# A diffusion layer on one core: the last modulation block by TensorE alone, and GLA's steps of a head moved

## The chip, the cores and the metric

The kernel runs on one core of one Trainium2 chip. The metric is device time in microseconds, from the start to the end of one execution; three runs of the kernel before gave 1934.57 to 1935.82 us, median 1935.3. The engines of a core have their own instruction streams and wait for each other by semaphores: TensorE (PE, matmuls; PEld, its weight loads), VectorE (DVE), ScalarE (ACT), GpSimd (POOL) and SyncE (SP), which here issues most of the DMA transfers.

## The reference, cut to what matters

One layer of a hybrid diffusion model for 128 context tokens and 256 latent tokens, 384 in all, with 2048 channels, all in float32.

```python
mod = silu(cond) @ w_ada + b_ada                  # cond (2, 2048), w_ada (2048, 12288)
sh1, sc1, ga1, sh2, sc2, ga2 = split(mod, 6)      # six modulation vectors of 2048
h = rmsnorm(x, norm_pre_mix) * (1 + sc1) + sh1
proj = h @ w_in                                   # q, k, v, g, two low ranks, Fourier
o = gla(q, k, v, low ranks)                       # 4 heads, forward and backward scans
o = rmsnorm_head(o) * gla_out_norm * silu(g)
f = real(fft2(fo))                                # Fourier branch
g_a, g_b = split(sigmoid(h @ w_gate + b_gate))
m = (g_a * (o @ w_br_gla) + g_b * (f @ w_br_four)) @ w_out
x = x + ga1 * rmsnorm(m, norm_post_mix)
h = rmsnorm(x, norm_pre_ffn) * (1 + sc2) + sh2
x = x + ga2 * rmsnorm((silu(h @ w_g) * (h @ w_u)) @ w_d, norm_post_ffn)
```

GLA is a chunked scan. For each head it needs `q_in`, `k_in`, `k_out` from a cumulated decay, the products `k_in q_in` inside a chunk (the kernel's `at`), the products `k_out v` that update the state (`dl`), and the output (`po`).

## The kernel before, in words

The activations are held with the channels on the 128 partitions, as 16 tiles of 384 tokens. A float32 product is done as three matmuls on parts of less precision: each weight tile of 128 x 1024 (512 KB, `raw`) is loaded by SP, ACT makes the upper part `whi` (L256), DVE the rest `wlo` (L257), and PE does `whi` times `A_hi`, `whi` times `A_lo` and `wlo` times `A_hi` (L291). One such weight tile gives a **unit** of 24 matmuls of 384 columns. `grab` takes the oldest split tile and has the next one split, so that some three units of weights are ready ahead; `raw` has two buffers, `whi` and `wlo` four.

The stages, in order: the first two modulation vectors and the projection to v (`pv`, `pgm`), ending at some 145 us; q, k and the gates, with GLA beside them (146 to 420) and the Fourier input beside the rest (to 560); the **mix**, that is the projection to GLA's gate (`o`), the Fourier branch (`four`, tiles `pf`, `fd`, `y`) and GLA's branch (`a`) in an order written out in `mix_order` (to 745); the **output projection** with `w_out`, 32 units (745 to 890); then the feed-forward part, to the end.

Beside the units run Python generators: `step(side)` after each unit emits the next piece of a generator, up to its next `yield`. PE, ACT, DVE and POOL run in the order in which the code emits; SP's transfers are put in order by the scheduler, each as soon as its buffer can be free. The generators that matter here:

- `gla` (L756 and on): for each head the decay, then for each of two directions `qi`, `ki`, `ko` (DVE, L826 to L833), then a step with `at` and `cr` (PE, L850, L856) and `att` (DVE), a step with `am`, a step in which `kout` and `att` are split (`part`, `ap`, L318), then the states: a step for direction 0 and a step for direction 1, each with two products `dl` (PE) and `S` (ACT, DVE), then three steps with `po`.
- `ada_rest`: the modulation blocks (m, half) for m = 2, 3, 4, each of 16 **granules** of 512 KB of `w_ada`. A granule is two DVE operations over 128 x 1024 (`adacc`, L661; L659 for the first), which multiply it with the two condition columns and add; after 16 of them PE sums over the partitions with `selr` (L679), ACT copies (L684), and a step later PE transposes (`ptm`, L688) and DVE writes `mods`. The last block, (4, 1), is split before: granules 0 to 7 by DVE; 8 to 15 by PE, in two groups of four (`fetch` to four tiles that the feed-forward part uses later, `adax`, L638; `rounds`, 16 matmuls of 32 columns for a group, L645).
- `paced` runs that generator at `rate[0]` steps a unit: 1.0 beside GLA, 0.25 in the `o` units of the mix, 1.25 in the output projection. What is left is run out after the fourth last pair of units.

Of the kernel before, what the change touches and what calls it, by code (L numbers as in the profile page):

```python
# [107 lines left out]
def tile_step(ctx: ExitStack, tc: tile.TileContext, a, o):  # L108
# [516 lines left out]
    spare_at = []  # L625

    def ada_rest(todo):
        for m in todo:
            for half in range(2):
                acc = adap.tile([P, 2, 1024], F32, tag="adacc", name="adacc")  # L630
                by_pe = KT // 2 if (m, half) == (todo[-1], 1) else 0
                ws = []

                def fetch(k0):

                    for n, t in enumerate(("hid_hi", "hid_lo", "S0", "S1")):
                        w = spare_at[0].tile([P, G], F32, tag=t, name="adax", bufs=1)
                        SP.dma_start(w, a["w_ada"][m - 2, half, k0 + n])  # L638
                        ws.append(w)

                def rounds(pr, k0):
                    for k in range(k0, k0 + 4):
                        w = ws.pop(0)
                        for j in range(4):
                            PE.matmul(  # L645
                                pr[32 * j : 32 * j + 32, :], spare_at[1][:, k, :], w[:, j * 256 : (j + 1) * 256],
                                start=k == by_pe, stop=False,
                            )

                if by_pe:  # L650
                    while not spare_at:
                        yield
                    fetch(by_pe)
                for k in range(by_pe or KT):
                    w = adap.tile([P, 1024], F32, tag="adaw", name="adaw", bufs=2)
                    SP.dma_start(w, a["w_ada"][m - 2, half, k])
                    for c in range(2):
                        if k == 0:
                            DVE.tensor_scalar_mul(acc[:, c, :], w, cond[:, k, c : c + 1])  # L659
                        else:  # L660
                            DVE.scalar_tensor_tensor(  # L661
                                acc[:, c, :], w, cond[:, k, c : c + 1], acc[:, c, :], op0=ALU.mult, op1=ALU.add,
                            )
                    if by_pe and k == 4:
                        pr = pss.tile([P, 256], F32, tag="side", name="pr")
                        rounds(pr, by_pe)
                        fetch(by_pe + 4)
                    yield
                yield
                if m == todo[-1]:  # L670
                    yield
                    yield
                if by_pe:
                    rounds(pr, by_pe + 4)
                else:
                    pr = pss.tile([P, 256], F32, tag="side", name="pr")
                for c in range(2):
                    for j in range(4):
                        PE.matmul(  # L679
                            pr[32 * j : 32 * j + 32, :], selr[:, 32 * c : 32 * c + 32],  # L680
                            acc[:, c, j * 256 : (j + 1) * 256], start=c == 0 and not by_pe, stop=c == 1,
                        )
                ev = acc[:, 0, 0:256]
                ACT.copy(ev, pr)  # L684
                yield
                pt = pss.tile([P, 2, P], F32, tag="side", name="ptm")
                for b in range(2):
                    PE.transpose(pt[:, b, :], ev[:, b * P : (b + 1) * P], ident)  # L688

                src = pt.rearrange("p b (j r) -> p j b r", r=32)  # L690
                mh = mods[:, m, 8 * half : 8 * half + 8, :]
                for c in range(2):
                    DVE.tensor_copy(mh[:, :, c].rearrange("p (j b) -> p j b", b=2), src[:, :, :, c])
                bc = lambda v: v[:, 8 * half : 8 * half + 8].unsqueeze(2).to_broadcast([P, 8, 2])
                DVE.tensor_add(mh, mh, bc(bsc1[:, 1, :] if m == 4 else cols[:, m, :]))
                w1 = {2: 1, 4: 2, 5: 3}.get(m)
                if w1 is not None:
                    DVE.tensor_mul(mh, mh, bc(norms[:, w1, :]))
# [10 lines left out]
    ada_gen = ada_rest((2, 3, 4))  # L709
# [13 lines left out]
    with ExitStack() as s:  # L723
# [28 lines left out]
        def gla():  # L752
# [10 lines left out]
            for h in range(NH):  # L763
# [80 lines left out]

                ats = []
# [47 lines left out]
                for d in range(2):  # L893
# [13 lines left out]
                    yield  # L907
# [57 lines left out]
    with ExitStack() as s:  # L965
# [229 lines left out]
        sd = side()  # L1195
        mT, late = None, []
        for b, i in mix_order:
            if b == "o":
# [9 lines left out]
                rate[0] = 0.25  # L1208
                step(sd)
                rate[0] = 0.0  # L1210
# [24 lines left out]
    with ExitStack() as s:  # L1235
# [16 lines left out]
        spare_at.extend([pe, cpad])  # L1252
# [22 lines left out]
        def wout_last(p, i):  # L1275
# [6 lines left out]
            ACT.activation(sq2, mg32(i), AF.Square)  # L1282
            return sq0, pr, sq2

        rate[0] = 1.25
        spare_h = {-4: ((pe, "hid_hi", 1), (pe, "hid_lo", 1)), -2: ((pe, "S0", 1), (pe, "S1", 1))}
        spare_w = ((adap, "adaw", 2), (adap, "adaw", 2))
        raw2 = None
        for i in range(KT):
# [28 lines left out]
            if i == KT - 4:  # L1318
                for _ in ada_gen:
                    pass  # L1320
# [894 lines left out]
```

## Time and profile before

| what | value |
|---|---|
| median of three runs | 1935.3 us |
| the profiled execution, and its span | 1936.34 us, 1934.3 us |
| PE busy, share of the span | 1902.8 us, 98% |
| DVE busy, share of the span | 1652.6 us, 85% |
| ACT busy, share of the span | 1079.1 us, 56% |
| DMA, mean rate | 225 GB/s |
| `adacc` on DVE (L661) | 164 operations, 202.7 us |
| granules loaded for DVE (`adaw`), for PE (`adax`) | 88, 8 |

The profile is one execution on the chip; its times count from the start of the span. Busy times of one engine overlap with those of the others. A row of waits names the waiting engine and tile, then what released it. Idle time of an engine that is not the bottleneck costs nothing by itself. The granted clock is the share of PE's full clock that the chip allowed.

### The profile page before, as it was taken

The page shows a single profiled execution, that of the slowest core. Times are in us where ns is not written, and L with a number is a line of the kernel's source. Part 1 is how long each engine was busy: PE and PEld are TensorE (multiplying, and loading weights), DVE is VectorE, ACT ScalarE, POOL GpSimd, SP SyncE. Part 2 cuts the span into 40 slices and gives each one's busy share as a digit, 9 for nine tenths or more (in the row PEclk, how much of TensorE's full clock was granted, in tenths as well). Part 3 has the DMA queues.
Part 4 walks back from the last instruction along what each step waited for, and adds up shares of the span by engine and source line. Part 5 has one row for each costly group of instructions (what it writes and reads, how often), then busy time and mean ns, then how long its engine had stood idle before and what let it go on. Part 6 is the DMA issues. An engine that isn't in the chain of part 4 may idle for free.

```text
span 1934.3 us, 27966 instructions
## 1 busy us (share of the span) xinstructions
PE 1902.8 (98%) x10348; PEld 1676.3 (87%) x10348; DVE 1652.6 (85%) x2120; ACT 1079.1 (56%) x1569; POOL 160.0 (8%) x189
## 2 busy tenths in 40 slices
PE   8999999999999999999999999999999999999997
PEld 5779999999999899899988888888888888888886
DVE  5677898778958897988799999999999999988985
ACT  4335445454346554346456666767576666666554
POOL 0000001000000000003000111111112021111001
PEclk9999999999999999999999999999999999999999
DMA  9986777787756788665639696978888797959563
GB/s 389 372 317 214 241 222 222 232 273 242 249 167 198 242 265 278 222 237 168 214 109 272 165 275 155 258 183 237 204 221 228 191 245 183 260 133 265 142 225 94
DMA packets 247529, 435.66 MB, mean 225 GB/s; under 512 B 45916, under 2 KB 150556, under 8 KB 242784
## 3 DMA queue, kind: packets, MB, share of 16 engines
q1 hardware_dynamic: 199792, 391.59, 60.7%
q0 software_dynamic: 18944, 33.63, 11.6%
q10 hardware_dynamic: 28656, 8.65, 2.6%
q8 instruction: 81, 1.33, 0.3%
q14 instruction: 56, 0.46, 0.1%
HBM read 369.05 MB, written 57.67 MB: 221 GB/s over the span
## 4 chain that ended last, share of the span: by engine, by line
PE 81%; DVE 8%; DMA 6%; ACT 3%; issue 2%; SPq 0%; POOL 0%; ACTq 0%; DVEq 0%
PE pgu L1731 31%; PE pmm L291 20%; PE pdn L1731 10%; PE pds L1731 7%; PE pv L449 3%; DVE adacc L661 2%; DVE wlo L257 2%; PE pgm L432 1%; PE pfo L1096 1%; ACT whi L256 1%; DMA raw<-in_w_out 1%; DMA slab<-in_w_ada 1%; DMA raw<-in_w_br_gla 1%; DMA raw<-in_w_in 1%; PE px L467 1%
## 5 line engine op out<-in xcount | busy, mean ns | idle before, releaser
L291 PE MATMUL pmm<-A_hi,wlo 128*128 128x384 f32 x1072 | 359.7, 336 | 4.0 <-DVE wlo L257 4.0
L291 PE MATMUL pmm<-A_hi,whi 128*128 128x384 f32 x1072 | 362.7, 338 | 0.0
L291 PE MATMUL pmm<-A_lo,whi 128*128 128x384 f32 x1072 | 359.2, 335 | 0.0
L1629 ACT CAST whi<-u 128x1024 fp32r<-128x1024 f32 x200 | 210.4, 1053 | 173.2 <-PE pds L1731 40.5
L1640 DVE TENSOR_TENSOR wlo<-u,whi 128x1024 fp32r<-128x1024 f32 x200 | 243.9, 1220 | 35.1 <-ACT whi L1629 30.8
L256 ACT CAST whi<-raw 128x1024 fp32r<-128x1024 f32 x163 | 170.4, 1050 | 183.1 <-DMA raw<-in_w_gate 68.8
L1731 PE MATMUL pgu<-whi,A_hi 128*128 128x512 f32 x640 | 249.9, 390 | 0.0
L1731 PE MATMUL pgu<-whi,A_lo 128*128 128x512 f32 x640 | 249.1, 389 | 0.0
L257 DVE TENSOR_TENSOR wlo<-raw,whi 128x1024 fp32r<-128x1024 f32 x161 | 196.1, 1221 | 48.7 <-ACT whi L256 43.5
L1629 ACT CAST whi<-raw 128x1024 fp32r<-128x1024 f32 x157 | 165.0, 1053 | 87.5 <-PE pgu L1731 25.7
L291 PEld LDWEIGHTS pmm<-A_hi,wlo 128*128 128x128 f32 x1072 | 201.7, 188 | 5.1 <-DVE wlo L257 5.0
L291 PEld LDWEIGHTS pmm<-A_hi,whi 128*128 128x128 f32 x1072 | 201.7, 188 | 4.6 <-issue 3.0
L661 DVE SCALAR_TENSOR_TENSOR adacc<-adaw,cond,adacc 128x1024 f32<-128x1024 f32 x164 | 202.7, 1278 | 3.0 <-DMA adaw<-in_w_ada 2.8
L291 PEld LDWEIGHTS pmm<-A_lo,whi 128*128 128x128 f32 x1072 | 201.9, 188 | 0.2
L1640 DVE TENSOR_TENSOR wlo<-raw,whi 128x1024 fp32r<-128x1024 f32 x157 | 191.3, 1219 | 10.6 <-ACT whi L1629 10.1
L1731 PE MATMUL pgu<-wlo,A_hi 128*128 128x512 f32 x640 | 185.8, 389 | 0.0
L1731 PEld LDWEIGHTS pgu<-whi,A_hi 128*128 128x128 f32 x640 | 120.1, 188 | 25.9 <-issue 0.8
L1731 PEld LDWEIGHTS pgu<-wlo,A_hi 128*128 128x128 f32 x640 | 120.1, 188 | 25.1
L1731 PEld LDWEIGHTS pgu<-whi,A_lo 128*128 128x128 f32 x640 | 120.1, 188 | 24.7
L1731 PE MATMUL pgu<-whi,S 128*128 128x512 f32 x400 | 116.6, 389 | 0.0
L1864 POOL DMA_DIRECT2D sums_d<-spare x64 | 58.3, 945 | 622.8 <-ACT spare L1860 601.6
L1731 PE MATMUL pdn<-whi,hid_hi 128*128 128x512 f32 x264 | 102.8, 389 | 0.0
(462 smaller groups left out, 3541.6 us busy)
## 6 DMA issues: line engine op xcount, KB each, us to landing
adaw<-in_w_ada SPq DMA_DIRECT2D x88, 512.0 KB, 4.4
raw<-in_w_d SPq DMA_DIRECT2D x70, 512.0 KB, 5.7
slab<-in_w_ada SPq DMA_DIRECT2D x32, 1024.0 KB, 10.7
raw<-in_w_gate SPq DMA_DIRECT2D x64, 512.0 KB, 4.9
raw<-in_w_g SPq DMA_DIRECT2D x48, 512.0 KB, 3.7
raw<-in_w_u SPq DMA_DIRECT2D x48, 512.0 KB, 4.4
u<-in_w_u SPq DMA_DIRECT2D x40, 512.0 KB, 5.4
u<-in_w_g SPq DMA_DIRECT2D x40, 512.0 KB, 8.4
```

The lines of the kernel that those rows point to most:

```text
L256: ACT.copy(hi, raw)
L257: sub = lambda: eng.tensor_sub(lo, raw, hi.bitcast(F32))
L291: PE.matmul(dst, w[wi][:, k * n + n0 : k * n + n0 + P], x[xi][:, k0 + k, :], start=first and k == 0 and j == 0, stop=last and k == kts - 1 ...
L432: PE.matmul(pgv[q : q + 32, :], spad[:, k, :], slab[k // (KT // 2)][:, k % (KT // 2), :], start=k < 4, stop=k >= KT - 4,)
L449: PE.matmul(pv[2 * t + g], hT[x_][:, kb, t * P : (t + 1) * P], w_[:, g * 512 : (g + 1) * 512], start=kb == 0 and j == 0, stop=kb == KT - 1 ...
L467: PE.matmul(px, w_[:, u * P : (u + 1) * P], hT[x_][:, kb, :], start=j == 0, stop=j == 2)
L661: DVE.scalar_tensor_tensor(acc[:, c, :], w, cond[:, k, c : c + 1], acc[:, c, :], op0=ALU.mult, op1=ALU.add,)
L1096: PE.matmul(p, w[0][:, c], x[:, 0 : 2 * n], start=kh == k == 0, stop=False)
L1629: ACT.copy(hi, src)
L1640: DVE.tensor_sub(lo, src, hi.bitcast(F32))
L1731: PE.matmul(dst, stat[x_][m], mov(w[w_], m), start=first and w_ == m == x_ == 0, stop=last and w_ == m == 1, skip_group_check=any(more),)
L1864: POOL.dma_start(sums_d[k], u, accum_op=ALU.add)
```

## The change

Three edits:

1. The last modulation block (4, 1) is done by PE alone: a new generator `ada_pe` loads its 16 granules in four groups of four and multiplies each group six units later. `ada_rest` has the other five blocks only.
2. The mix has no modulation steps (`rate` is 0 there). In the output projection `ada_rest` runs at 0.8 steps a unit, for all 16 granules of block (4, 0), and `ada_pe` beside it with one step a unit.
3. In GLA a `yield` is added ahead of `at`, and the `yield` between the state products of the two directions is taken out, so that a head has as many steps as before.

```diff
-    def ada_rest(todo):
-        for m in todo:
-            for half in range(2):
...
-                by_pe = KT // 2 if (m, half) == (todo[-1], 1) else 0
...
-                    if by_pe and k == 4:
-                        pr = pss.tile([P, 256], F32, tag="side", name="pr")
-                        rounds(pr, by_pe)
-                        fetch(by_pe + 4)
-                    yield
+    def ada_rest(blocks):
+        for m, half in blocks:
...
+    def ada_pe(pool, cpad, ev, m, half, apart):
+
+        def fetch(k0):
+
+            ws = []
+            for n, t in enumerate(("hid_hi", "hid_lo", "S0", "S1")):
+                ws.append(pool.tile([P, G], F32, tag=t, name="adax", bufs=1))
+                SP.dma_start(ws[n], a["w_ada"][m - 2, half, k0 + n])
+            return ws
+
+        pr = None
+        for k0 in range(0, KT, 4):
+            ws = fetch(k0)
+            for _ in range(apart):
+                yield
+            if pr is None:
+                pr = pss.tile([P, 256], F32, tag="side", name="pr")
+            for n, w in enumerate(ws):
+                for j in range(4):
+                    PE.matmul(
+                        pr[32 * j : 32 * j + 32, :], cpad[:, k0 + n, :], w[:, j * 256 : (j + 1) * 256],
+                        start=k0 + n == 0, stop=k0 + n == KT - 1,
+                    )
+        yield from ada_finish(m, half, pr, ev)
...
-    ada_gen = ada_rest((2, 3, 4))
+    ada_gen = ada_rest([(m, half) for m in (2, 3, 4) for half in range(2)][:-1])
...
                     dec.append((tot, dc))
                     yield
 
+                yield
                 ats = []
...
                             S[d] = split2((f"Sh{d}", f"Sl{d}"), new)
-                    yield
+                yield
                 for t in range(3):
...
         sd = side()
+        rate[0] = 0.0
         mT, late = None, []
...
-                rate[0] = 0.25
                 step(sd)
-                rate[0] = 0.0
...
-        spare_at.extend([pe, cpad])
+        by_pe = ada_pe(pe, cpad, pd.tile([P, 256], F32, name="evp", bufs=1), 4, 1, 6)
...
-        rate[0] = 1.25
+        rate[0] = 0.8
...
                 step(ada)
+                step(by_pe)
             if i == KT - 4:
-                for _ in ada_gen:
-                    pass
+                for gen in (ada_gen, by_pe):
+                    for _ in gen:
+                        pass
```

`ada_finish` holds the copy, the transposes and the writes to `mods` that stood at the end of `ada_rest`.

How the order moves, at three places. First DVE in GLA's head 0, from the `wlo` behind the last `ki` chain to the split of `kout` (`part<-ko`); before:

```order
L257 TENSOR_TENSOR wlo<-raw,whi 128x1024
L860 COPY_PREDICATED att<-mask,at 64x3x64 x2
L661 SCALAR_TENSOR_TENSOR adacc<-adaw,cond,adacc 128x1024 x2
L257 TENSOR_TENSOR wlo<-raw,whi 128x1024
L872 COPY_PREDICATED am<-mask,at 128x192
L875 TENSOR_TENSOR att<-att,am 64x3x64 x2
L880 TENSOR_TENSOR qi<-qi,eb 128x2x64 x2
L661 SCALAR_TENSOR_TENSOR adacc<-adaw,cond,adacc 128x1024 x2
L257 TENSOR_TENSOR wlo<-raw,whi 128x1024
L318 TENSOR_TENSOR part<-ko,part 128x256 x2
```

and with the change:

```order
L257 TENSOR_TENSOR wlo<-raw,whi 128x1024
L652 SCALAR_TENSOR_TENSOR adacc<-adaw,cond,adacc 128x1024 x2
L257 TENSOR_TENSOR wlo<-raw,whi 128x1024
L854 COPY_PREDICATED att<-mask,at 64x3x64 x2
L652 SCALAR_TENSOR_TENSOR adacc<-adaw,cond,adacc 128x1024 x2
L257 TENSOR_TENSOR wlo<-raw,whi 128x1024
L866 COPY_PREDICATED am<-mask,at 128x192
L869 TENSOR_TENSOR att<-att,am 64x3x64 x2
L874 TENSOR_TENSOR qi<-qi,eb 128x2x64 x2
L652 SCALAR_TENSOR_TENSOR adacc<-adaw,cond,adacc 128x1024 x2
L257 TENSOR_TENSOR wlo<-raw,whi 128x1024
L318 TENSOR_TENSOR part<-ko,part 128x256 x2
```

One more pair `adacc` and one more `wlo` now stand ahead of `att`, and so ahead of all that follows in the head. Second, DVE at the states of the same head (`S`, and `part<-S` for its split); before:

```order
L903 SCALAR_TENSOR_TENSOR S<-s_1602,dc,dl 128x256
L318 TENSOR_TENSOR part<-S,part 128x256
L661 SCALAR_TENSOR_TENSOR adacc<-adaw,cond,adacc 128x1024 x2
L257 TENSOR_TENSOR wlo<-raw,whi 128x1024
L903 SCALAR_TENSOR_TENSOR S<-s_1604,dc,dl 128x256
L318 TENSOR_TENSOR part<-S,part 128x256
L661 SCALAR_TENSOR_TENSOR adacc<-adaw,cond,adacc 128x1024 x2
```

and with the change:

```order
L897 SCALAR_TENSOR_TENSOR S<-s_1602,dc,dl 128x256
L318 TENSOR_TENSOR part<-S,part 128x256
L897 SCALAR_TENSOR_TENSOR S<-s_1604,dc,dl 128x256
L318 TENSOR_TENSOR part<-S,part 128x256
L652 SCALAR_TENSOR_TENSOR adacc<-adaw,cond,adacc 128x1024 x2
```

The two directions stand together; the work of one unit that stood between them is now in front of the head's later steps. Third, SP in the output projection, with the loads of `w_out` (`raw`) and of granules for DVE (`adaw`) and for PE (`adax`); before, from its start:

```order
L214 DMA raw<-in_w_out 128x1024 x3
L638 DMA adax<-in_w_ada 128x1024 x3
L214 DMA raw<-in_w_out 128x1024
L656 DMA adaw<-in_w_ada 128x1024
L214 DMA raw<-in_w_out 128x1024
L638 DMA adax<-in_w_ada 128x1024
L656 DMA adaw<-in_w_ada 128x1024
L214 DMA raw<-in_w_out 128x1024
L656 DMA adaw<-in_w_ada 128x1024
```

and with the change, from the same place through its second group:

```order
L214 DMA raw<-in_w_out 128x1024 x3
L675 DMA adax<-in_w_ada 128x1024 x4
L214 DMA raw<-in_w_out 128x1024 x2
L647 DMA adaw<-in_w_ada 128x1024
L214 DMA raw<-in_w_out 128x1024
L647 DMA adaw<-in_w_ada 128x1024
L214 DMA raw<-in_w_out 128x1024
L647 DMA adaw<-in_w_ada 128x1024
L214 DMA raw<-in_w_out 128x1024
L647 DMA adaw<-in_w_ada 128x1024
L214 DMA raw<-in_w_out 128x1024
L675 DMA adax<-in_w_ada 128x1024 x4
```

A group of `adax` is now four loads in a row, and comes again with six loads of `raw` between; the later groups stand behind the matmuls that free their tiles.

More of the change, by code (lines that the diff above doesn't have):

```diff
@@ new lines, in ada_finish @@
+    def ada_finish(m, half, pr, ev):
+        ACT.copy(ev, pr)
+        yield
+        pt = pss.tile([P, 2, P], F32, tag="side", name="ptm")
+        for b in range(2):
+            PE.transpose(pt[:, b, :], ev[:, b * P : (b + 1) * P], ident)
+        src = pt.rearrange("p b (j r) -> p j b r", r=32)
+        mh = mods[:, m, 8 * half : 8 * half + 8, :]
+        for c in range(2):
+            DVE.tensor_copy(mh[:, :, c].rearrange("p (j b) -> p j b", b=2), src[:, :, :, c])
+        bc = lambda v: v[:, 8 * half : 8 * half + 8].unsqueeze(2).to_broadcast([P, 8, 2])
+        DVE.tensor_add(mh, mh, bc(bsc1[:, 1, :] if m == 4 else cols[:, m, :]))
+        w1 = {2: 1, 4: 2, 5: 3}.get(m)
+        if w1 is not None:
+            DVE.tensor_mul(mh, mh, bc(norms[:, w1, :]))
@@ L843, in gla @@
                     yield
+                yield
                 ats = []
@@ L906, in gla @@
                             S[d] = split2((f"Sh{d}", f"Sl{d}"), new)
-                    yield
+                yield
                 for t in range(3):
```

76 lines of the change are left out of this document (20 added, 56 removed).

## The prediction

> **What bounds the kernel now.** I read the page first, for the shares of the engines.
>
> ```profile
> PE 1902.8 (98%) x10348; PEld 1676.3 (87%) x10348; DVE 1652.6 (85%) x2120; ACT 1079.1 (56%) x1569; POOL 160.0 (8%) x189
> ```
>
> TensorE (PE) is idle for 1934.3 - 1902.8 = 31.5 us of the span. The change can win only by removing idle time of PE, or time in which PE runs at a lower clock, and it loses by whatever it adds to PE's own work. So the next view is the list of PE's waits over the whole span.
>
> ```profile
> PE at L850 <- DVE ki L827: 5.8, 3, 3.0
> PE pmm L291 <- DVE wlo L257: 4.0, 3, 2.8
> ...
> PE pf L1171 <- DVE wlo L257: 2.7, 5, 0.8
> ...
> PE pmm L291 <- DVE fd L1175: 1.3, 1, 1.3
> PE ptm L688 <- ACT adacc L684: 1.0, 1, 1.0
> ```
>
> The columns are the sum in us, the number of waits and the longest one. These five rows hold 14.8 us, and each lies in a stage that the change touches: `at` in GLA, `pf` and `fd` in the mix, `wlo` in the mix and the output projection, `ptm` in the output projection. The rest of the idle time, at the start and the end of the program, stays. I now take the three stages one by one.
>
> **GLA: one more unit ahead of `at`.** First a row of the chain of waits from a stretch without breaks, for the length of a unit; then the timeline of PE at head 0, and the busy time by windows over the same place (the last three figures of a row are the granted clock, the DMA share and GB/s):
>
> ```profile
> 824.69 25.18 PE pmm L291 x144
> ...
> 191.18 0.57 PE L850 MATMUL at<-qi,ki 128*64 128x64 f32 x12
> 194.79 0.57 PE L850 MATMUL at<-qi,ki 128*64 128x64 f32 x12 [3.04 <-DVE ki L827]
> ...
> 191.00:194.50 3.50, 0.74 (x14) 0.43 (x12) 3.50 (x5) 1.47 (x3) 0.00 (x0) 1.00 0.48 125
> 196.20:199.50 3.30, 3.30 (x13) 3.29 (x12) 3.29 (x5) 1.04 (x2) 0.00 (x0) 0.52 0.47 128
> ```
>
> PE does the `at` products of direction 0, then waits 3.04 us for direction 1. VectorE (DVE) is busy all through that window (3.50 of 3.50), so it is behind. The wait has a tail: from 196.2 to 199.5 the granted clock is 0.52, and 13 matmuls run where a full clock gives 3.30 / 0.175 = 19, so some six are missing; at 0.52 of the clock (1 - 0.52) x 3.30 = 1.6 us are lost. Head 0 loses 3.04 + 1.6 = 4.6 us. A unit (24 matmuls of a projection) takes 25.18 x 24 / 144 = 4.2 us on PE, 0.175 a matmul, and the new `yield` puts one whole unit between `ki` and `at`. 4.2 is over 3.04, so this wait goes.
>
> What is late next is `dl`, which needs the split of `kout` (tile `part`). Two steps of the chain of waits give the pitch of DVE's work, and the timeline around `dl` the margin:
>
> ```profile
> 190.18 2.39 DVE adacc L661 x2
> 192.57 1.13 DVE wlo L257
> ...
> 208.29 0.75 DVE L318 TENSOR_TENSOR part<-ko,part 128x256 fp32r<-128x256 f32 x2
> ...
> 209.98 0.88 PE L761 MATMUL dl<-vr,part 128*128 128x256 f32 x6
> ```
>
> By the order of instructions DVE does one more pair `adacc` and one more `wlo` ahead of `part`: 2.39 + 1.13 = 3.5 us. DVE has no gap here, so the first `part` ends at 208.7 + 3.5 = 212.2. PE, without the wait, reaches `dl` at 191.18 + 4.2 (the added unit) + 1.5 (`at` twice and `cr`, some 0.5 each) + 12.5 (three units at the full clock) = 209.4. The first two of its products need only the upper part; the third waits, from about 209.6 to 212.2: **2.6 us of the 4.6 come back as a new wait, 2.0 are won.** The rest of the head holds: the states of both directions in one step put one `S` and one `part`, 0.4 us each by the row of `part`, a unit earlier. From the end of the wait PE needs 1.1 (the other ten products of `dl`) + 2 x 4.2 + 0.4 (the first `po`) = 9.9 us to the first product that reads them. DVE needs 0.5 + 2.39 + 1.13 for `ap`, `adacc` and `wlo`, then four splits and two states with their splits, eight operations of 0.4 to 0.5, and some 0.5 of waiting for ScalarE at each of the last two: about 8.5. It is near, but covered; where it is not, the price is at most the 0.8 us for each head.
>
> Heads 2 and 3 wait 1.38 us each (5.8 is 3.04 + 2 x 1.38); head 1 does not wait.
>
> ```profile
> 313.47 0.57 PE L850 MATMUL at<-qi,ki 128*64 128x64 f32 x12
> 315.42 0.57 PE L850 MATMUL at<-qi,ki 128*64 128x64 f32 x12 [1.38 <-DVE ki L827]
> ...
> 328.94 0.75 DVE L318 TENSOR_TENSOR part<-ko,part 128x256 fp32r<-128x256 f32 x2
> ...
> 329.02 1.13 PE L761 MATMUL dl<-vr,part 128*128 128x256 f32 x6
> ```
>
> Head 2 in the same way: `part` at 329.4 + 3.5 = 332.9, PE's third product at 313.47 + 4.2 + 1.5 + 12.5 + 0.2 = 331.9, a new wait of 1.0. Gone are 1.38 and the 0.25 us by which this `dl` is longer than that of head 0. Won: 0.6, and as much in head 3. GLA in sum: 2.0 + 0.6 + 0.6 = **3.2 us**. Ends: 7.4 (the 5.8 and the 1.6 all go, if DVE is not late at `dl`), and 1.6 if the new wait of head 0 costs the clock again.
>
> On that clock the trace has two cases: the wait of 3.04 us was followed by a low clock, and the longest wait of the output projection, 2.8 us, was not:
>
> ```profile
> PE pmm L291 <- DVE wlo L257: 3.4, 2, 2.8
> ...
> 780.00:800.00 20.00, 16.60 (x94) 15.96 (x94) 19.78 (x22) 7.51 (x13) 0.00 (x0) 1.00 0.70 231
> ```
>
> The new wait of 2.6 us is nearer to the second, so I charge nothing and keep 1.6 us for the range. [...]
>
> **The mix: no modulation work.** Of the waits quoted above, those on `pf` (2.7) and on `fd` (1.3) lie between 600 and 690. The third that PE has there, the busy time of the instructions on `adacc` in these 90 us, and the chain of waits at one of the places:
>
> ```profile
> PE pmm L291 <- DVE wlo L257: 0.6, 1, 0.6
> ...
> 600.00:690.00 90.00, 0.00 (x0) 0.00 (x0) 7.42 (x6) 0.00 (x0) 1.00 0.72 238
> ...
> 634.58 2.48 DVE adacc L661 x2
> 637.05 1.14 DVE wlo L257
> 638.19 0.03 DVE fd L1175
> 638.21 4.62 DMA raw<-in_w_in
> ```
>
> PE waits 2.7 + 1.3 + 0.6 = 4.6 us in all. DVE spends 7.42 us on three pairs of `adacc` here, and the chain shows what a pair does: it holds `wlo`, that holds the buffer of the next load, and this load lands 4.62 us later. The pairs go, with their loads, and the work with them moves to the output projection. I take 4.0 of the 4.6 us: the chain runs through the pairs at 611, 634 and 666, but behind 671 it runs through transfers of `yb` that stay. Ends: 1.3 (the one wait on `fd`, whose pair stands directly ahead of it) and 4.6 (all of it). A loss is excluded, since nothing is added in this stage.
>
> **The output projection.** The chain of waits in its second half:
>
> ```profile
> 822.83 1.86 PE pr L645 x32
> ...
> 849.88 1.86 PE pr L645 x32
> 851.74 0.86 PE pr L679 x16
> ```
>
> PE's work: a group of four granules is 1.86 us (32 records are 16 matmuls of 32 columns). There were two groups and there will be four: +3.7. The selecting matmuls L679 of the last block go: -0.9. The transposes `ptm` of one block come here from the mix, no change in sum. Added: **+2.8 us**.
>
> PE's waits between 745 and 890: 3.4 us for `wlo` and 1.0 for `ptm`, by the rows above. The group rows of DVE between 752.5 and 782 give the reason for the first:
>
> ```profile
> L661 DVE SCALAR_TENSOR_TENSOR adacc<-adaw,cond,adacc 128x1024 f32<-128x1024 f32 x14 | 17.2, 1279 | 0.2 <-DMA adaw<-in_w_ada 0.2
> L257 DVE TENSOR_TENSOR wlo<-raw,whi 128x1024 fp32r<-128x1024 f32 x6 | 7.3, 1221 | 2.0 <-ACT whi L256 2.0
> L1272 DVE TENSOR_TENSOR qs<-qs,pr 128x384 f32<-128x384 f32 x2 | 1.1, 558 | 0.1
> ```
>
> At a rate of 1.25 granules a unit, DVE does 1.25 x 2 x 1.28 + 1.22 + 1.1 (four operations of 0.55 us for every two units) = 5.5 us a unit, against 4.2 on PE. At 0.8 it is 2.05 + 1.22 + 1.1 = 4.4, while PE with its added matmuls takes (26 x 4.2 + 7.4 + 0.9 + 0.7) / 26 = 4.5. DVE no longer falls behind, and its 3.4 us go. The `ptm` wait came from two generator steps in one unit (the copy, then at once the transpose that reads it); at 0.8, and with one step a unit for the other generator, a unit lies between them, so 1.0 goes too. Won: 4.4 - 2.8 = 1.6.
>
> The new loads: SyncE's order has three groups of four `adax` in mid-stage, each of them behind the matmuls that free its tiles, and loads of `raw` and `adaw` behind the group. The trace has one such group:
>
> ```profile
> L638 SPq DMA_DIRECT2D adax<-in_w_ada x8: 328/432/634, 752.3 to 826.3; - x8
> ...
> DMA to landing us min/median/max: 6.0/6.9/7.9
> L656 SPq DMA_DIRECT2D adaw<-in_w_ada x88: 327/328/422, 157.0 to 839.6; - x88
> ...
> DMA to landing us min/median/max: 3.4/4.4/6.6
> ...
> 826.27 2.48 DVE L661 SCALAR_TENSOR_TENSOR adacc<-adaw,cond,adacc 128x1024 f32<-128x1024 f32 x2 [0.90 <-DMA adaw<-in_w_ada]
> 831.52 2.48 DVE L661 SCALAR_TENSOR_TENSOR adacc<-adaw,cond,adacc 128x1024 f32<-128x1024 f32 x2 [1.63 <-DMA adaw<-in_w_ada]
> ```
>
> It made DVE wait 0.90 + 1.63 = 2.5 us, and a load in its company takes 6.9 us and not 4.4, 2.5 us more. PE did not wait behind it (144 matmuls without a break): the weights split ahead covered it. I charge nothing for the first two groups and 0.6 us in all for the reserve being smaller here. The stage: 1.6 - 0.6 = **1.0 us** won. Ends: 1.6, and 1.6 - 3 x 5.0 = -13.4 if no group is covered; the row of 144 matmuls is by far the nearer.
>
> **The sum.** 3.2 + 4.0 + 1.0 = 8.2 us. The profiled execution took 1936.3 us (1934.3 of span and 2.0 around it), 1.0 more than the median of the runs shown, 1935.3. It becomes 1928.1, and the median 1927.1.
>
> **The rivals.**
> - *The waits in GLA all go.* DVE would have to be ahead at `dl`. Against it: no gap of DVE at head 0. It gives 7.4 in place of 3.2, so 1922.9.
> - *The new wait costs the clock.* For it: the row at 196.2. 1.6 us less won: 1928.7.
> - *The waits only move.* `dl` takes all that `at` gave in heads 2 and 3 and the clock falls in head 0 (0.4 us won), the mix keeps the waits that stand behind no pair of its own (1.3 won), the output projection gives 0.5: 2.2 us, 1933.1, no change that can be told. Against it: the chain runs through the pairs themselves.
> - *The groups of loads are not covered: slower.* Each of the three groups makes PE wait 5.0 us (2.5 for DVE's wait and 2.5 for the late `raw`), since the weights split ahead are fewer than at 823. 3 x 5.0 = 15.0 us against 3.2 + 4.0 + 1.6 = 8.8: 1941.5. It turns the sign from 8.8 / 3 = 2.9 us a group. For it: `wlo` is already late at 783 and 795 in this stage. Against it: there DVE was overloaded, and will not be.
>
> **Chances.** Forecast 0.50; all waits of GLA go 0.10; the clock 0.18; the waits only move 0.13; slower 0.09. A measurement of this kernel tells about 0.2%, 3.9 us, from no change. Faster by more: 0.50 + 0.10 + 0.18 = 0.78; within: 0.13; slower: 0.09. The range reaches down to the case in which every term stands at its good end, 7.4 + 4.6 + 1.6 = 13.6 us (1921.7), and up to the waits that only move; it leaves out the slower case: from 1921.5 to 1933.0.
>
> **What would show it.** In PE's waits: no row `at` on `ki`; a new row `dl` on `part`, 2 to 3 us in head 0 and about 1 in heads 2 and 3; `pf` and `fd` together under 1 us; no `ptm`; `wlo` in the output projection under 1 us. In the windows: a clock of 1.00 from 190 to 215. The group `pr` on `adax` has 128 records. The prediction is wrong if `dl` waits as long as `at` did, if the mix still shows 2 us or more of waits, or if PE waits for `wlo` behind each group of loads.

## The result, and the profile after

| kernel | median (us) | executions | ratio to before, 95% interval |
|---|---|---|---|
| before, same chip | 1934.95 (1934.57 to 1935.82) | 4 | |
| after | 1924.13 (1923.67 to 1924.93) | 4 | 0.9944 (0.9927 to 0.9961) |

The change makes the kernel 10.8 us faster. The ratios below are of executions at the usual clock: one of `states_together`, 3147.7 us at a granted clock of 0.56, is left out of them. The forecast was 1927.1 us with a range of 1921.5 to 1933.0: the sign and the range held, and the gain is 2.6 us larger than the 8.2 forecast. Section 1 of the page after:

```profile
PE 1900.5 (99%) x10396; PEld 1676.3 (87%) x10396; DVE 1634.0 (85%) x2104; ACT 1079.3 (56%) x1569; POOL 160.3 (8%) x189
```

The span is 1923.2 us, so PE's idle time fell from 31.5 to 22.7 us, 8.8 us less. The span is 11.1 us shorter; PE's busy time fell by 2.3 us too, although it has 48 matmuls more: what is counted as busy holds some waiting, of which more below. The list of PE's waits after (sum, number, longest), cut to the stages of the change, shows the first part:

```profile
PE dl L754 <- DVE part L318: 4.2, 3, 2.0
...
PE pf L1165 <- DVE wlo L257: 0.9, 1, 0.9
...
PE pfo L1091 <- DVE wlo L318: 0.4, 1, 0.4
```

`at` on `ki` is gone and `dl` on `part` has come, as the prediction said; `pf` has one wait in place of five; `fd`, `ptm` and `wlo` are gone. The group of the PE-made modulation block (duration min/median/max, first and last start) and its loads:

```profile
L687 PE MATMUL pr<-adax,cpad x128: 379/379/403, 766.0 to 850.1; 128*32 128x256 f32 x128
L675 SPq DMA_DIRECT2D adax<-in_w_ada x16: 328/420/1924, 741.9 to 822.1; - x16
...
DMA to landing us min/median/max: 5.8/6.3/6.5
```

To see where the time went, lists of waits aren't enough, so I put the two traces side by side by the start of each unit's first product (every 24th matmul of L291). The table gives how many us **after** is ahead of **before** at the end of each stage, and what the stage added:

| stage (time in before) | ahead at its end | added | forecast |
|---|---|---|---|
| ahead of GLA (146) | 0.1 | 0.1 | 0 |
| GLA (to 420) | 2.8 | 2.7 | 3.2 |
| Fourier input (to 600) | 2.5 | -0.2 | 0 |
| mix (to 733) | 8.8 | 6.3 | 4.0 |
| output projection (to 878) | 10.5 | 1.6 | 1.0 |
| the rest | 11.1 | 0.7 | 0 |

The 0.7 at the end is not the change: behind the wait of 2.4 us on `bk`, which both kernels have, the clock is low in before (0.50 from 1923.5 to 1926.9) and not in after (1.00), and the 16 matmuls that follow take 3.53 us in before and 1.97 in after (the last section has the windows).

### The profile page after: what moved, and what is told of

The parts are those of the page before. It is cut to its first block, busy times and chain, and to the rows that moved or that the text cites. A ratio compares the mean times of both kernels' runs of the same rounds, so it can differ in the third digit from the quotient of the medians.

```text
span 1923.2 us, 28041 instructions
## 1 busy us (share of the span) xinstructions
PE 1900.5 (99%) x10396; PEld 1676.3 (87%) x10396; DVE 1634.0 (85%) x2104; ACT 1079.3 (56%) x1569; POOL 160.3 (8%) x189
## 4 chain that ended last, share of the span: by engine, by line
PE 87%; DVE 6%; ACT 2%; DMA 2%; issue 2%; SPq 0%; POOLq 0%; POOL 0%; ACTq 0%; DVEq 0%
PE pgu L1726 31%; PE pmm L291 25%; PE pdn L1726 10%; PE pds L1726 7%; PE pv L449 3%; DVE adacc L652 2%; PE pgm L432 1%; DVE wlo L257 1%; PE pfo L1090 1%; DMA slab<-in_w_ada 1%; PE px L467 1%; PE pmm L1440 1%; PE pf L1164 1%; PE pfo L1091 1%; PE po L754 1%
## 5 line engine op out<-in xcount | busy, mean ns | idle before, releaser
L291 PE MATMUL pmm<-A_hi,whi 128*128 128x384 f32 x1072 | 362.5, 338 | 0.0
L291 PE MATMUL pmm<-A_hi,wlo 128*128 128x384 f32 x1072 | 358.9, 335 | 0.0
L291 PE MATMUL pmm<-A_lo,whi 128*128 128x384 f32 x1072 | 358.8, 335 | 0.0
L291 PEld LDWEIGHTS pmm<-A_hi,whi 128*128 128x128 f32 x1072 | 201.5, 188 | 5.4 <-issue 3.9
L291 PEld LDWEIGHTS pmm<-A_lo,whi 128*128 128x128 f32 x1072 | 201.6, 188 | 0.2
L291 PEld LDWEIGHTS pmm<-A_hi,wlo 128*128 128x128 f32 x1072 | 201.4, 188 | 0.1
L652 DVE SCALAR_TENSOR_TENSOR adacc<-adaw,cond,adacc 128x1024 f32<-128x1024 f32 x150 | 185.6, 1279 | 3.6 <-DMA adaw<-in_w_ada 3.4
## 6 DMA issues: line engine op xcount, KB each, us to landing
slab<-in_w_ada SPq DMA_DIRECT2D x32, 1024.0 KB, 10.8
```

Source lines behind the costliest of these rows:

```text
L291: PE.matmul(dst, w[wi][:, k * n + n0 : k * n + n0 + P], x[xi][:, k0 + k, :], start=first and k == 0 and j == 0, stop=last and k == kts - 1 ...
L652: DVE.scalar_tensor_tensor(acc[:, c, :], w, cond[:, k, c : c + 1], acc[:, c, :], op0=ALU.mult, op1=ALU.add,)
```

## Experiments: the change taken apart

**The two halves.** `gla_alone` is the kernel before with the third edit only; `mod_alone` is the kernel after with GLA as before.

```diff
 # gla_alone, against before
+                yield
                 ats = []
...
-                    yield
+                yield
```

Expected of the first: 

> The kernel before with the GLA edit alone (one more yield ahead of at, the states of both directions in one step). Read from the profile with the change, unit by unit, this edit is worth 2.7 us: 1.3 in head 0, 0.7 each in heads 2 and 3. Theory A (the waits on ki go, and part of each comes back as a wait of dl on part): 1932.2 us, PE's waits show no at, and dl 2.0 + 1.1 + 1.1. Rival (what GLA won was owed to work that left the other stages): within 0.5 us of 1934.9.

Expected of the second: 

> The kernel with the change, with GLA as before. Theory A (the edits add up): 10.8 - 2.7 = 8.1 us under the kernel before, 1926.8 us; at waits 5.8 us again in three waits, dl does not wait, and the mix and the output projection look as in the kernel with the change. Rival (the earlier end of GLA gives the mix part of its gain): 1928 us or more, with over 2 us of waits in the mix.

Measured: `gla_alone` 1932.66 us (11 executions; ratio 0.9994, 0.9986 to 1.0003), 1.7 us under the 1934.38 of before on that chip; `mod_alone` 1926.33 (5; ratio 0.9956, 0.9944 to 0.9968), 8.0 us under it. By unit starts `mod_alone` gains 6.3 us in the mix and 1.6 in the output projection, the very figures of after. Within the spread the two halves add up (1.7 + 8.0 = 9.7), and the modulation half carries 8.0 of the 10.8 us. GLA's share alone can't be told from nothing by the times.

**The mix alone and the change without it.** `mix_back` is after with the quarter rate put back into the mix; `mix_only` is before with that rate taken out and nothing else.

```diff
 # mix_back, against after (in the o units)
+                rate[0] = 0.25
                 step(sd)
+                rate[0] = 0.0
...
 # mix_only, against before
+        rate[0] = 0.0
...
-                rate[0] = 0.25
                 step(sd)
-                rate[0] = 0.0
```

Expected of `mix_back`:

> The kernel with the change, with the four modulation steps put back into the mix (rate 0.25 in its o units); the output projection keeps 0.8 steps a unit and the PE block. Theory A (a pair of adacc delays wlo and with it the next load, so PE waits): the mix loses the 6.3 us that it won by the unit starts, 1930.4 us, with pf and fd waiting 4 to 5 us in sum and each wait behind a pair of adacc. Rival (the waits in the mix came from the loads in its company or from the place of the last block, not from DVE): under 1926 us.

Expected of `mix_only`:

> The kernel before with rate 0 in the mix and nothing else: `ada_rest` as before with its last block split between DVE and PE, 1.25 steps a unit in the output projection, the remainder run out at its end. Theory: the mix wins its 6.3 us between the unit starts, as in the kernel after, but the four granules that it gave up come to an output projection in which DVE is already overloaded (5.5 us a unit against 4.2): four pairs of 2.55 us, about 10 us of DVE, of which PE sees what is left at the end, 4 to 8 us, as waits on `wlo` and at the run-out (`ptm`, `pr`). Net -2 to +2 us: 1932.5 to 1936.5. Rival: DVE has room for them at the end of the output projection, and the mix's 6.3 us are won alone: 1928 to 1929.

Measured: `mix_back` 1932.45 us (12; ratio 0.9991, 0.9983 to 0.9999), `mix_only` 1935.06 (12; ratio 1.0005, 0.9996 to 1.0013) against 1934.19. By unit starts the mix gains nothing in `mix_back` (-0.04 us) and 6.3 in `mix_only`: the mix's gain is due to those granules. Whether it is their work on DVE or their loads, these two runs don't tell apart, since both go together; that it is the work rests on the chain of waits in the prediction. But `mix_only` gives it all back, -7.8 us in its output projection. PE's waits there:

```profile
PE pmm L291 <- DVE wlo L257: 4.3, 2, 2.3
...
PE ptm L688 <- ACT adacc L684: 2.9, 2, 2.3
```

These are 7.2 us, where before has 4.4, and each of the three longest is followed by a low clock in its trace (the mean granted clock of this execution is 0.995, that of before 0.997). With the 1.6 us that the prediction puts on a low clock, an estimate is 7.2 - 4.4 + 3 x 1.6 = 7.6 us, near the 7.8. So the second edit is worth nothing without the first: the block given to PE makes the room that the four granules of the mix need. The theory for `mix_only` held. That for `mix_back` held in the mechanism; its median is 2 us above the 1930.4 expected, with executions from 1930.55 to 1938.53.

**The output projection: rate and grouping.** `rate125` and `rate100` are after with 1.25 and 1.0 steps a unit in place of 0.8; `apart3` has the groups of loads three units apart in place of six.

```diff
 # rate125 (rate100: 1.0)
-        rate[0] = 0.8
+        rate[0] = 1.25
...
 # apart3
-        by_pe = ada_pe(pe, cpad, pd.tile([P, 256], F32, name="evp", bufs=1), 4, 1, 6)
+        by_pe = ada_pe(pe, cpad, pd.tile([P, 256], F32, name="evp", bufs=1), 4, 1, 3)
```

Expected of `rate125`:

> The kernel with the change, with ada_rest at 1.25 steps a unit in the output projection as before, and nothing else changed. Theory A (at 1.25 DVE has 5.5 us of work for a unit of 4.2 to 4.5 us, so it falls behind): PE waits again for wlo, 2 to 4 us, and for ptm by 1 us: 1926.5 to 1928.5 us. Rival (the weights split ahead cover 16 granules at any pace; the gain came from the smaller number of granules): within 0.5 us of 1924.1, no wait of PE in this stage but ptm.

Expected of `rate100`:

> The kernel after with `ada_rest` at 1.0 steps a unit in the output projection in place of 0.8 (1.25 gave 1940.8, with 7.7 us in one wait of `ptm` where copy and transpose fell into one unit, and low clocks). Theory: what broke 1.25 is the two steps in one unit and DVE at 5.5 us a unit; at 1.0 no unit has two steps and DVE needs 2.55 + 1.22 + 1.1 = 4.9 us a unit against PE's 4.5, some 0.4 x 20 = 8 us behind at the end of the blocks, of which the weights split ahead cover the most: 1924 to 1927, no `ptm` wait over 1 us. Rival: any rate at which DVE falls behind empties the reserve and calls late loads behind the groups of four: over 1928, with `wlo` waits of 3 us or more.

Expected of `apart3`:

> The kernel after with the four groups three units apart in place of six. It tests whether spreading the groups matters. While the groups last (12 units of 4.5 us, 54 us), the loads are 12 of `raw`, 9 to 10 of `adaw` and 16 of `adax`, some 38 of 524 KB: 19.9 MB in 54 us, 370 GB/s, where no window of 20 us in the traces so far showed more than 300. Theory: PE waits for late `raw` (through `whi` and `wlo`) some 5 to 12 us in the first half of the output projection, 1929 to 1936. Rival: the transfers of the tiles are loaded far enough ahead, and the groups cost only their 1.86 us each: within 1 us of the kernel after, 1923 to 1925.

Measured: `rate125` 1940.83 us (5; ratio 1.0032, 1.0020 to 1.0044), `rate100` 1926.42 (5) beside 1925.96 for after on the same chip, `apart3` 1925.71 (4). PE's waits of `rate125`:

```profile
PE ptm L630 <- ACT adacc L626: 7.7, 1, 7.7
...
PE pmm L291 <- DVE wlo L257: 2.0, 2, 1.8
```

and the end of its chain of waits ahead of the long one:

```profile
803.63 2.40 DVE adacc L652 x2
...
806.04 0.02 issue
806.05 0.33 SPq L647
...
806.48 0.38 SPq L675
...
806.91 6.58 DMA raw<-in_w_out
...
815.89 3.54 DMA raw<-in_w_out
```

At 1.25 DVE ends a pair late, at 806.0, and frees a granule's buffer with it. SP issues that granule's load (L647), then one for PE (L675), and only then the load of `raw` that stands behind them in its order; it lands after 6.58 us. A later load of `raw` takes its buffer, is issued at 815.9 and lands at 819.4. On ScalarE the copy of the block's sum stands, in the order of the code, behind the split of that later load, which starts at 819.5, and the copy runs at 822.0. PE meets the transpose of the copy in the same unit and stands for 7.7 us; the clock is low (0.50) for 10.24 us from 816.7, and the stage ends 5.4 us behind before instead of 10.5 ahead of it. My expectation (1926.5 to 1928.5) missed this by 12 us: I had counted DVE's overload and not a copy that is caught in ScalarE's order.

At 1.0, with never two steps in a unit, no `ptm` wait appears, `wlo` waits 0.5 us once, and the median is 0.5 us over that of after: the theory held. By unit starts its output projection wins 1.1 us, against 1.6 in after. The rate of 0.8 isn't a sharp choice; the fall lies between 1.0 and 1.25.

Groups three units apart cost nothing that the times can tell. The theory of 5 to 12 us fell; its rival held in the mechanism, with a median 0.7 us above its 1923 to 1925. The windows show why: after already moves more in its busiest window of this stage than I had allowed for, and `apart3` needs no more than that. My limit of 300 GB/s was a misreading, too: before itself has 319 from 660 to 680 and 308 from 820 to 840.

```profile
795.00:815.00 20.00, 20.00 (x116) 20.00 (x117) 18.82 (x22) 8.44 (x13) 0.00 (x0) 1.00 0.89 323
```

```profile
775.00:795.00 20.00, 20.00 (x137) 18.82 (x136) 17.70 (x22) 6.22 (x11) 0.00 (x0) 1.00 0.85 327
```

(first row after, second `apart3`; the last figure is GB/s.) The 16 loads of `apart3` were issued within 45 us and PE waited for none of them; the stage shows one wait, 1.2 us on the copy ahead of `ptm` at the end of the PE-made block, and by unit starts it wins 0.2 us where after wins 1.6.

## Experiments: GLA, and a version that beats both

**Only the merging.** `states_together` has the second half of the third edit on the kernel before.

```diff
-                    yield
+                yield
```

Expected of `states_together`:

> The kernel before with only the second half of the third edit: the states of both directions in one step, no added step ahead of `at`. Theory: this half saves nothing by itself, it only gives back the step that the other half adds. The three `at` waits stay at 5.3 to 5.8 us, the low clock behind the wait of head 0 may come or not, and the median is within 1.0 us of the kernel before on the same chip. Rival: a part of the 2.7 us that GLA won between the unit starts comes from the merging (fewer steps to the first `po`): 1 us or more faster. A second rival: `po` waits for the splits of `S`, which now stand behind one another: 0.5 to 2.4 us slower, with a row `po` on `part`.

Measured 1934.92 us (ratio 1.0005, 0.9996 to 1.0014): nothing. The `at` waits stay, at 4.3 us in this profile and not the 5.3 to 5.8 expected, and there is no wait of `po`.

**The new wait taken away in two ways.** `part_early` splits `kout` in the added step; `rate75` leaves the order and takes some 3.5 granules out of DVE's way ahead of head 0; `part_rate` does both; `after_again` is after itself, beside the last two.

```diff
 # part_early, against after
                 yield
+                kp = [split2((f"koh{d}", f"kol{d}"), kout[d]) for d in range(2)]
                 ats = []
...
-                kp = [split2((f"koh{d}", f"kol{d}"), kout[d]) for d in range(2)]
...
 # rate75, against after
-        rate[0] = 1.0
+        rate[0] = 0.75
         for i in QK[1:]:
             proj(psm, hT, keep(qk, i), sd)
+        rate[0] = 1.0
```

Expected of `part_early`:

> The kernel after, with the splits of `kout` (`part<-ko`) emitted in the added step, ahead of `at`, so that on DVE they stand two pairs `adacc` and two `wlo` earlier. Theory: the new waits of `dl` on `part` (2.0 + 1.1 + 1.1 us in the profile after) are only a matter of DVE's order, so they go, and with the first of them the low clock at 211.6 (3.41 us at about half, 1.6 us). DVE's work is the same. The median is 4.2 to 5.8 us under the kernel after run beside it (1924.1 alone): 1918.3 to 1920. Rival: DVE is behind by a fixed amount, and the wait moves on to the next product of the head (`po` on the splits of `S` or `ap`): the time stays within 1.5 us of the kernel after, 1922.6 to 1925.6, with a new row of 3 us or more in PE's waits.

Expected of `after_again`:

> The kernel after, unchanged, as the measure for the three kernels beside it on this chip (and for the runs with early splits, whose median of 1923.5 us came from another chip than the 1924.1 us of the kernel after). Theory: 1924.1 us within 0.7 us; waits of `dl` on `part` 4 to 5.5 us; a low clock of 3.41 us behind the wait of head 0 in some executions and not in others.

Expected of `rate75`:

> The kernel after with `ada_rest` at 0.75 steps a unit in place of 1.0 in the units of q and k (146 to some 230 us), then 1.0 as before: some 3.5 granules, 3.5 x 2.5 = 9 us of DVE, leave the time ahead of head 0's end and come back behind 536 us, where DVE is busy 5 us in 10. Theory: DVE is simply behind by its amount of work in head 0, so the wait of `dl` there (2.0 us, and 1.6 us for the clock) goes: 2.0 to 3.6 us won, while heads 2 and 3 keep their 1.1 us each; 1920.5 to 1922 against 1924.1. Rival: it is the order that counts (`part` stands behind the pair of its own step), the wait of head 0 stays at over 1 us, and the median stays within 1 us.

Expected of `part_rate`:

> Both of the edits that take a wait away: the splits of `kout` ahead of `at`, and the rate of 0.75 in the units of q and k. With the early splits alone the 4.9 us won at `dl` in head 0 fell back to 1.5 at the first `bT` of head 1, behind a chain of `adacc` and `wlo`, a late load of `raw` and the logarithm on ScalarE. Theory: with 9 us less of DVE work that chain starts earlier and the 2.6 to 3.3 us at `bT` are won as well: 1919 to 1921, under the kernel after and under the early splits alone. Rival: the chain at `bT` is bound by the load and by ScalarE and not by DVE; then it gives 1922.5 to 1924, as the early splits alone.

| kernel | median (us) | ratio to before, 95% interval | ahead of before at head 0's end / GLA's end / the end |
|---|---|---|---|
| after | 1924.13 | 0.9944 (0.9927 to 0.9961) | 1.4 / 2.8 / 11.1 |
| part_early | 1923.53 (1923.00 to 1925.77) | 0.9945 (0.9934 to 0.9957) | 4.2 / 5.4 / 13.1 |
| after_again | 1925.96 (1923.29 to 1927.65) | 0.9952 (0.9939 to 0.9966) | 0.8 / 2.3 / 10.7 |
| rate75 | 1924.21 (1921.74 to 1926.02) | 0.9942 (0.9929 to 0.9954) | 4.3 / 5.4 / 10.1 |
| part_rate | 1923.02 (1920.63 to 1923.09) | 0.9934 (0.9921 to 0.9946) | 4.9 / 9.3 / 13.0 |

(The last column is from the one profiled execution of each.)

`part_early`: all three waits of `dl` are gone, and 1.0 to 1.4 us more than in after is kept in each of heads 2 and 3. Head 0's gain of some 3 us is not: in the unit that starts at 239.7 in before, the lead falls from 4.2 to 1.5 us. The timeline and the chain of waits there (the piece of 1.28 us is a table load of ScalarE ahead of the logarithm):

```profile
240.39 0.33 PE L803 MATMUL bT<-cg,lah 128*128 128x128 f32 x1 [0.50 <-ACT lah L317]
...
241.38 0.33 PE L803 MATMUL bT<-cg,lal 128*128 128x128 f32 x1 [0.67 <-DVE lal L318]
```

```profile
224.33 2.48 DVE adacc L652 x2
226.81 1.15 DVE wlo L257
227.97 4.66 DMA raw<-in_w_gate
...
236.22 1.28 ACT L787
237.52 0.85 ACT la L787
238.40 1.03 DVE la L789 x2
```

The chain runs through DVE's pairs, a late load, ScalarE's split and logarithm, to the decay of head 1. Behind these 1.2 us the closing sum of a block, `pr`, waits 0.7 us more for DVE's `adacc`. This is the rival in head 0 (a fixed lag of DVE that moves to the next product that needs it) and the theory in heads 2 and 3; the median, 1923.53, lies in the rival's range and not in the theory's.

`after_again` shows how far one kernel moves: its waits of `dl` (4.7 us) came as expected, and the low clock with them, but its median is 1.8 us above the 1924.1, where I had allowed 0.7.

`rate75`: less DVE work ahead of head 0 cuts its wait to 0.5 us (lead 4.3 us, and no fall at `bT`), so it was the amount as much as the order; `dl` waits 3.0 us in all. But it gives 2.3 us back in the Fourier input stage (a wait of 1.9 us of `bnp` with a low clock behind it), and its median, 1924.21, is within 1 us of 1924.1, as its rival had it. With both edits PE waits nowhere from 146 to 400, and GLA ends 9.3 us ahead of before. But `part_rate` then gives 1.9 us back in the Fourier input stage:

```profile
420.43 0.26 DVE L984 TENSOR_TENSOR wn<-wnr 128x64 f32<-128x64 f32 x1
...
420.79 0.54 PE L991 MATMUL bnp<-fx,wn 128*32 128x194 f32 x8 [1.93 <-issue]
```

```profile
418.40:421.81 3.41, 1.48 (x14) 0.88 (x13) 3.41 (x5) 2.53 (x3) 0.55 (x2) 1.00 0.81 289
421.81:425.23 3.42, 3.42 (x13) 3.42 (x12) 3.42 (x5) 0.00 (x0) 0.00 (x0) 0.50 0.99 373
```

PE now arrives at the products of `bnp` ahead of their input, waits 1.93 us, and pays a low clock behind it. The row names no releaser, but `wn`, which these products read, ends on DVE at 420.7, just ahead of them, and stands there behind a pair `adacc` that ends at 420.5, so it is most likely DVE that is late once more. What was put off, one granule and the closing sum of a block, comes into the output projection, which gives -0.4 us where after gives +1.6, with a `ptm` wait of 0.8 us. The net is 2.9 us under after on the same chip: all five executions of `part_rate` (highest 1923.09) lie under all five of `after_again` (lowest 1923.29). It is the fastest version here, clearly under before and narrowly under after. Its median is 2 us over the 1919 to 1921 expected and in its rival's range (1922.5 to 1924): the gain at `bT` came, as the theory had it, and was in part lost behind it. For `part_early` and `rate75` alone the times can't tell a gain.

## Why the prediction was right or wrong

- **GLA, 3.2 forecast, 2.7 between the two profiles.** The mechanism was right. `part` ended where DVE's order put it:

```profile
209.82 1.22 DVE L257 TENSOR_TENSOR wlo<-raw,whi 128x1024 fp32r<-128x1024 f32 x1
...
210.96 0.75 DVE L318 TENSOR_TENSOR part<-ko,part 128x256 fp32r<-128x256 f32 x2
...
211.43 1.95 PE L754 MATMUL dl<-vr,part 128*128 128x256 f32 x8 [2.02 <-DVE part L318]
```

  PE came to the third product at 209.4 (forecast 209.6) and waited to 211.4 (forecast 212.2): 2.0 us in place of 2.6. Heads 2 and 3 wait 1.1 each, against 1.0. What failed is the sentence "I charge nothing" for the clock: the rival came true, as the windows of after show.

```profile
208.18:211.59 3.41, 1.39 (x9) 1.19 (x8) 3.41 (x5) 1.27 (x2) 0.00 (x0) 1.00 0.45 148
211.59:215.01 3.42, 3.42 (x15) 3.42 (x16) 3.42 (x5) 2.43 (x7) 2.66 (x5) 0.50 0.88 330
```

  The price of 1.6 us was about right, the chance of 0.18 was not (last section), and the clock of 1.00 from 190 to 215 that was to show the forecast isn't there. And the term rested on one execution of before, in which head 0 waited 3.04 us and the clock fell: the same order in `mod_alone` waits 2.5 us, in `mix_only` at most 1.7, and in neither does the clock fall there. These two traces, without the edit, won 2.0 and 2.9 us in GLA against before's profile, no less than the 2.7 of after. So it is luck that 3.2 and 2.7 lie so near, and a gain by the GLA edit isn't shown clear of the spread; the medians of the halves put it at 1.2 to 2.8 us (`gla_alone` 1.7 under before, after and `after_again` 2.8 and 1.2 further under it than `mod_alone`).

- **The mix, 4.0 forecast, 6.3 measured.** The mechanism was right (`mix_back`), the size was read from the wrong view. The step that failed is "PE waits 2.7 + 1.3 + 0.6 = 4.6 us in all". The rows of the weight loads (PEld) over the same stage of before, 600 to 680, and of after, were there to be read:

```profile
PEld pf L1171 <- DVE wlo L257: 4.4, 6, 1.1
PEld pmm L291 <- DVE fd L1175: 1.5, 1, 1.5
PEld pmm L291 <- DVE wlo L257: 0.9, 1, 0.9
PEld pf L1170 <- ACT whi L256: 0.3, 1, 0.3
```

```profile
PEld pf L1165 <- DVE wlo L257: 1.2, 1, 1.2
```

  They give 7.1 - 1.2 = 5.9 us. A product of 384 columns is on record for 0.33 us while one starts every 0.175 us, so at each wait PE's row counts the tail of the product ahead, some 0.16 us, as busy, and two of the nine waits don't appear in it at all. In all the list shows (7.1 - 4.6) / 9 = 0.3 us too little for each of the nine on the mean. In its own terms the forecast of 4.0 was good: by PE's lists 4.6 - 0.9 = 3.7 us went. The wait that I expected to stay, behind 671, did stay: 0.9 us at 670 in after, which is 679 in before.

- **The output projection, 1.0 forecast, 1.6 measured.** The 1.6 of won waits less added matmuls came out, four times alike (after, `after_again`, `mod_alone`, `part_early`: 1.65 us each), but as the difference of two terms that were both too small. The rows of the weight loads from 733 to 890, in before and in after:

```profile
PEld pmm L291 <- DVE wlo L257: 4.0, 2, 3.1
PEld ptm L688 <- ACT adacc L684: 1.3, 1, 1.3
PEld pmm L291 <- issue: 1.2, 3, 0.4
PEld pr L645 <- issue: 0.5, 2, 0.2
```

```profile
PEld pmm L291 <- issue: 1.6, 4, 0.4
PEld pr L687 <- issue: 0.9, 4, 0.3
```

  By them the waits that went are 4.0 + 1.3 = 5.3 us and not 4.4. The added work then cost some 5.3 - 1.65 = 3.7 us and not 2.8; the rows with `issue`, 2.5 us in after and 1.7 in before, show 0.8 of the difference; these gaps stand at the groups and at the sums. The 0.6 us charged for a smaller reserve behind the groups was not needed; PE has no `wlo` wait there. The rival of uncovered groups fell: their loads land in 6.3 us by the median, but PE doesn't wait. `rate125` shows that its danger is real, at the rate that the change left behind.

- **Not in the sum.** The Fourier input stage lost 0.2 us, net of a wait of `pfo` (0.4), and the end won 0.7 by the clock.

So the part of the gain that comes from the modulation work, 8.0 us by `mod_alone`, was placed rightly and sized too low, and GLA, where the argument was longest, brought what can't be told from the spread.

## What to carry to other kernels

Read what a wait costs from the weight loads' rows, or from the starts of equal units, not from PE's own rows: here nine short waits cost about 0.3 us each beyond what PE's list shows. Work for an engine that is late in one stage is worth moving only if the stage that receives it has been relieved first: the same edit gained 6.3 us in the mix both times, and kept them only beside the other. A wait that was removed from DVE while it was behind went here to the next product that needed it (`at` 3.0 us, `dl` 2.0, `bT` 1.2, `bnp` 1.9), until DVE's work itself was made less (0.5 us in head 0 of `rate75`).

## What the runs showed of the hardware

In each of 14 traces all changes of the granted clock after the first lie a whole number of 3.413 us from each other. In before the clock goes to 0.50 at 196.35 and at 1923.50, in after at 211.59 and at 1918.26: 506 and 500 times 3.4133 us. Over all windows of that length, laid as a grid from these changes, in all these traces between 20 and 1900 us (idle time of PE in the window, and whether the next one has the clock at 0.50):

```
idle 1.85 to 3.41 us: 16 windows, next one low in 16
idle 1.60 to 1.84 us:  7 windows, next one low in 1
idle under 1.60 us:    next one low in none
```

The 23 windows above 1.60 us come from few places of nearly equal kernels, so what they show near 1.85 us holds for waits of this kernel only. The prediction's two cases lie on its two sides: the wait of 3.04 us in head 0 of before put 1.85 us into the window ahead of the low one, while its wait of 2.8 us near 793 was cut by the grid into 1.2 and 1.6 us, and the clock stayed at 1.00:

```profile
790.27:793.69 3.42, 2.19 (x13) 1.87 (x11) 3.42 (x4) 1.51 (x3) 0.00 (x0) 1.00 0.43 103
793.69:797.10 3.41, 1.81 (x10) 1.81 (x11) 3.26 (x4) 1.07 (x3) 0.00 (x0) 1.00 0.79 268
```

The wait of 2.4 us on `bk` lies whole in one window in before and is cut into 0.9 and 1.5 us in after.

Two rows each of two kernels with the same order in GLA show the two sides. In `after_again` the wait of head 0 lies inside one window; in `gla_alone` a wait of 2.2 us is cut in two by the grid, and the clock stays.

```profile
209.30:212.72 3.42, 0.91 (x8) 0.71 (x8) 3.42 (x6) 1.67 (x3) 0.00 (x0) 1.00 0.40 125
212.72:216.13 3.41, 3.41 (x15) 3.41 (x14) 3.41 (x4) 1.65 (x5) 3.20 (x5) 0.50 0.91 306
```

```profile
209.91:213.32 3.41, 1.66 (x13) 1.66 (x14) 3.41 (x6) 2.40 (x5) 0.74 (x2) 1.00 0.59 184
213.32:216.74 3.42, 3.42 (x21) 3.42 (x20) 3.42 (x5) 0.93 (x4) 3.37 (x5) 1.00 0.95 253
```

The low window does 15 matmuls where the other does 21. From the 1.85 us and the 3.41 us of these windows, an estimate, with 1.85 us of idle time in one window taken as what costs the clock: a wait of 2.0 us, at a random place on the grid, has 1 - (2 x 1.85 - 2.0) / 3.41 = 0.5 to cost the clock, one of 2.5 us 0.65, and one of 3.0 us 0.8. In the seven traces with after's order in GLA the clock fell behind head 0 five times. The prediction gave 0.18.

Part of the spread between executions goes with the low windows. Six runs beside after have the same order in GLA as after. Against before's profile, which has one low window there, GLA won 3.6 and 2.7 us where no window was low (`mix_back`, `gla_alone`), 2.7, 2.3 and 1.8 with one (after, `after_again`, `rate100`), and 0.2 and 0.05 with two (`rate125`, `apart3`). The two traces with before's order and no low window there won 2.0 and 2.9 us (`mod_alone`, `mix_only`). A term of 3 us from one pair of profiles is no better than this, and the executions of one kernel lay 0.8 to 8 us apart.
